# Scores of a gated recurrence in four groups of products instead of eight, norm rows as one product, and mixer work moved from GpSimd to VectorE and ScalarE

## The chip, the cores and the metric

One core of one Trainium2 chip runs the kernel. The metric is the device time of one execution in microseconds, and the median of several runs is compared.

## What is computed

One inference step of a trunk of two layers, with a width of 1024, on 512 prompt tokens and 8 sample tokens. Each layer is a feed-forward block, a mixer of three parallel branches and a second feed-forward block, each with a norm before and after it. The change touches the mixer, above all its first branch (HGRN2, 4 heads of 128x128), and the norms:

```python
def gla_chunked(q, k, v, logf, s0):      # per head: S_t = diag(f_t) S_{t-1} + k_t v_t^T ; o_t = S_t^T q_t
    rel = jnp.where(mask, b[:, :, None] - b[:, None, :], -jnp.inf)   # b: running sum of logf in a chunk
    scores = jnp.einsum('bthk,btshk,bshk->btsh', qc, jnp.exp(rel), kc)
    o_intra = jnp.einsum('btsh,bshv->bthv', scores, vc)
    S_new = jnp.exp(b_last)[..., None] * S + jnp.einsum(
        'bshk,bshv->bhkv', kc * jnp.exp(b_last[:, None] - b), vc)
o = o * lax.rsqrt(jnp.mean(o * o, axis=-1, keepdims=True) + EPS)     # then the norm's gain and silu(xg)

def decoder_layer(x, ...):
    h = rms_norm(x, norm_g[0]);  x = x + 0.5 * rms_norm(swiglu(h, ...), norm_g[1])
    h = rms_norm(x, norm_g[2]);  proj = h @ w_in
    a_out = hgrn2_mixer(...);  b_out = gmlp_mixer(...);  c_out = s5_mixer(...)
    merged = sum of sigmoid gates * (branch @ w_branch);  x = x + rms_norm(merged @ w_out, norm_g[3])
    h = rms_norm(x, norm_g[4]);  x = x + 0.5 * rms_norm(swiglu(h, ...), norm_g[5])
```

The score of tokens t and s is a sum over the 128 key channels of q_t, k_s and the product of all forget gates f between s and t.

## The kernel before

**Layout.** Channels lie on the partitions and the 520 tokens on the columns, in two halves of 256 and 264. Each large product runs as three TensorE products on a high and a low part of both operands (`mm3`, lines 117 to 120). A weight unit of 128x1024 is loaded by SyncE into `raw`, cast to `whi` by ScalarE (L98), and its rest `wlo` is formed by VectorE (L102) or, with `share=True`, by GpSimd through `ptt` (L232).

**Order.** Each engine runs its instructions in order. The long products are the main line of the program; the recurrences are generators (`side`) that are moved on one step whenever `tick(us)` has counted enough time of products (3.1 us a step for a head, 2.0 us for the S5 scan). The chains of the four heads of a layer follow one another. The framework then lays the instructions out by its own estimates, so that the order on an engine isn't quite that of the text.

**A head** (`hgrn_operands`, `hgrn_head`). The projections give f, q and g, with two VectorE operations that scale f and k (L1003, L1004), and a GpSimd product for `sg`. The chain then makes the scores A: first the diagonal (L1030, L1031), then seven levels of doubling distance. Each level has four fp32 products of 64 columns (L1088), a GpSimd product that moves k on (L232), a VectorE product that moves q on (L1091) and a masked copy of 256 columns into A (L1092). The products T of the gates come from GpSimd. Between the levels, `load` brings the sample states of two tokens, `state` updates them with three GpSimd products (`st`, `vb`), and `output` multiplies them with q (L1071). After the levels come the transposes of k (L1106), the states (L1111), the output (L1123, L1125) and the norm of o.

**Norms.** `stat` sums squares with one-column products (L256, L258), `rstd` takes nine small VectorE steps (L220 to L228), and `rows` spreads the result over 128 partitions with two or three fp32 products (L270), one for each 128 tokens. There are 12 calls for the norms after a block, 12 for those before one, and 16 for the heads.

**S5 scan and gelu.** Each of 8 scan steps splits two products of 512 columns: VectorE takes one half, GpSimd the other (L812 to L835). `gelu2` takes three VectorE operations (L244, L245, L247).

## Time and profile before

| | us |
|---|---|
| median of 3 runs | 2754.24 |
| lowest and highest | 2752.72, 2756.12 |
| profiled execution, its own time | 2757.39 |
| span of its instructions | 2755.3 |
| VectorE, ScalarE, GpSimd busy in it | 1557.5, 1014.9, 795.2 |
| first mixer's heads 0 to 3 | about 480 to 700 from the start |
| second mixer's | about 1825 to 2045 from the start |

PE is TensorE's products, PEld its weight loads, DVE VectorE, ACT ScalarE, POOL GpSimd, SPq SyncE's queue. In a row of grouped instructions stand line, engine, operation, out<-in with shapes and count, then busy us and mean ns of one, then the idle time before them and what ended it. In a row in order of time stand start, length, engine, line and tiles, and in brackets the idle time before it. An fp32 product appears as two records, and a row with x8 is eight records; records overlap, so the pace is the length less one record, divided by seven. In a row by stretches stand the length and, for PE, PEld, DVE, ACT and POOL, busy time and number of instructions, then the granted share of TensorE's clock, the DMA share and GB/s. In a row of waits stand total, number and longest.

### The profile page before, as it was taken

The page shows a single profiled execution, that of the slowest core. Times are in us where ns is not written, and L with a number is a line of the kernel's source. Part 1 is how long each engine was busy: PE and PEld are TensorE (multiplying, and loading weights), DVE is VectorE, ACT ScalarE, POOL GpSimd, SP SyncE. Part 2 cuts the span into 40 slices and gives each one's busy share as a digit, 9 for nine tenths or more (in the row PEclk, how much of TensorE's full clock was granted, in tenths as well). Part 3 has the DMA queues.
Part 4 walks back from the last instruction along what each step waited for, and adds up shares of the span by engine and source line. Part 5 has one row for each costly group of instructions (what it writes and reads, how often), then busy time and mean ns, then how long its engine had stood idle before and what let it go on. Part 6 is the DMA issues. An engine that isn't in the chain of part 4 may idle for free. (4 is left out here: it accounts for less than half of the span.)

```text
span 2755.3 us, 54254 instructions
## 1 busy us (share of the span) xinstructions
PE 2673.8 (97%) x21976; PEld 2649.0 (96%) x21976; DVE 1557.5 (57%) x3127; ACT 1014.9 (37%) x2014; POOL 795.2 (29%) x1033
## 2 busy tenths in 40 slices
PE   7999999899999999999999999998999999999998
PEld 7999999889999999999999999998999999999998
DVE  7677867865574564344473434668555654634444
ACT  4344444333243353322343323433323334433232
POOL 5478812453221112011121101145521311301010
PEclk9999999999999999999999999999999999999999
DMA  4344543542232323232322222445332223222321
GB/s 135 102 141 148 160 135 121 182 126 83 86 93 92 116 77 93 93 92 100 93 77 93 90 95 93 131 135 156 98 100 86 87 92 120 84 89 88 99 91 54
DMA packets 131706, 291.16 MB, mean 106 GB/s; under 512 B 19024, under 2 KB 59760, under 8 KB 131456
## 3 DMA queue, kind: packets, MB, share of 16 engines
q1 hardware_dynamic: 131456, 287.70, 33.1%
q8 instruction: 173, 2.83, 0.4%
q14 instruction: 77, 0.63, 0.1%
HBM read 256.97 MB, written 30.67 MB: 104 GB/s over the span
## 5 line engine op out<-in xcount | busy, mean ns | idle before, releaser
L117 PE MATMUL mm<-h,whi 128*128 128x256 f32 (+1 forms) x4224 | 1057.9, 287 | 18.2 <-ACT h L298 7.0
L118 PE MATMUL mm<-h,wlo 128*128 128x256 f32 (+1 forms) x4224 | 1047.1, 284 | 1.1 <-DVE wlo L102 1.1
L117 PEld LDWEIGHTS mm<-h,whi 128*128 128x128 f32 x4224 | 801.6, 190 | 20.2 <-ACT h L298 7.0
L118 PEld LDWEIGHTS mm<-h,wlo 128*128 128x128 f32 x4224 | 804.0, 190 | 1.7 <-DVE wlo L102 1.6
L98 ACT CAST whi<-raw 128x1024 fp32r<-128x1024 f32 (+1 forms) x424 | 437.3, 1032 | 510.9 <-PE mm L120 432.7
L102 DVE TENSOR_TENSOR wlo<-raw,whi 128x1024 fp32r<-128x1024 f32 (+1 forms) x385 | 474.0, 1231 | 233.1 <-ACT whi L98 230.3
L120 PE MATMUL mm<-h,whi 128*128 128x256 f32 (+1 forms) x4224 | 594.5, 283 | 0.0
L120 PEld LDWEIGHTS mm<-h,whi 128*128 128x128 f32 x4224 | 543.1, 189 | 0.0
L111 POOL TENSOR_TENSOR hid<-vb,hid 128x256 fp32r<-128x256 f32 (+1 forms) x132 | 132.7, 1006 | 870.0 <-ACT hid L110 857.0
L117 PE MATMUL mm<-hid,whi 128*128 128x256 f32 (+1 forms) x1408 | 349.0, 284 | 3.6 <-ACT hid L110 3.6
L118 PE MATMUL mm<-hid,wlo 128*128 128x256 f32 (+1 forms) x1408 | 347.5, 283 | 0.0
L124 DVE TENSOR_TENSOR va<-mm,r 128x256 f32<-128x256 f32 (+1 forms) x320 | 136.1, 426 | 310.3 <-PE mm L120 304.0
L117 PEld LDWEIGHTS mm<-hid,whi 128*128 128x128 f32 x1408 | 265.6, 189 | 3.8 <-ACT hid L110 3.8
L118 PEld LDWEIGHTS mm<-hid,wlo 128*128 128x128 f32 x1408 | 266.2, 189 | 0.0
L120 PE MATMUL mm<-hid,whi 128*128 128x256 f32 (+1 forms) x1408 | 201.2, 283 | 0.3 <-DVE hid L111 0.3
L124 DVE TENSOR_TENSOR vb<-mm,r 128x256 f32<-128x256 f32 (+1 forms) x176 | 74.9, 425 | 192.5 <-PE mm L120 192.5
L120 PEld LDWEIGHTS mm<-hid,whi 128*128 128x128 f32 x1408 | 182.7, 189 | 0.5 <-DVE hid L111 0.5
L110 ACT CAST hid<-vb 128x256 fp32r<-128x256 f32 (+1 forms) x176 | 72.1, 410 | 280.4 <-DVE vb L403 277.1
L232 POOL TENSOR_TENSOR wlo<-raw,whi 128x1024 fp32r<-128x1024 f32 x39 | 94.8, 2432 | 226.5 <-ACT whi L98 226.5
L401 ACT ACTIVATE sil<-va 128x256 f32<-128x256 f32 (+1 forms) x176 | 73.7, 419 | 152.8 <-DVE va L124 149.1
L434 DVE TENSOR_TENSOR y<-mm,y 128x264 f32<-128x264 f32 (+1 forms) x128 | 54.2, 425 | 117.1 <-PE mm L120 116.6
L403 DVE TENSOR_TENSOR vb<-vb,sil 128x256 f32<-128x256 f32 (+1 forms) x176 | 83.6, 475 | 17.2 <-ACT sil L401 2.5
(462 smaller groups left out, 3792.2 us busy)
## 6 DMA issues: line engine op xcount, KB each, us to landing
raw<-in_w_up SPq DMA_DIRECT2D x176, 512.0 KB, 3.7
raw<-in_w_in SPq DMA_DIRECT2D x88, 512.0 KB, 3.6
raw<-in_w_down SPq DMA_DIRECT2D x64, 448.0 KB, 3.4
raw<-in_w_down SPq DMA_DIRECT2D x32, 512.0 KB, 3.5
tab<-tb SPq DMA_DIRECT2D x48, 256.0 KB, 2.3
tab<-tab SPq DMA_DIRECT2D x48, 256.0 KB, 3.4
raw<-in_w_branch SPq DMA_DIRECT2D x24, 512.0 KB, 3.7
raw<-in_w_out SPq DMA_DIRECT2D x16, 512.0 KB, 4.6
```

The source lines that it names most:

```text
L98: nc.scalar.copy(hi[:, :n], raw[:, :n])
L102: nc.vector.tensor_tensor(lo[:, :n], raw[:, :n], hi[:, :n].bitcast(F32), ALU.subtract)
L110: nc.scalar.copy(pair[:, 0], src)
L111: (lo_eng or nc.gpsimd).tensor_tensor(pair[:, 1], src, pair[:, 0].bitcast(F32), ALU.subtract)
L117: mm(out, wh, x[:, 0], start=first and k == 0, stop=False)
L118: mm(out, wl, x[:, 0], start=False, stop=False)
L120: mm(out, wh, x[:, 1], start=False, stop=last and k == n - 1)
L124: self.nc.vector.tensor_tensor(dst, p, self.rms(half), ALU.mult)
L232: self.nc.gpsimd.tensor_tensor(out, a, b, op)
L401: nc.scalar.activation(s, a, AF.Silu)
L403: nc.vector.tensor_tensor(b, b, s, ALU.mult)
L434: nc.vector.tensor_tensor(ys, pd, ys, ALU.add)
```

## The change

Seven things change; lines that only carry a new name are left out.

1. The scores come from four groups (the diagonal with level 0, then c = 2, 8, 32) instead of eight. Each group multiplies k with a widened q of 192 columns per 128 tokens (128 tokens and six segments), four products to a group, in two PSUM tiles. Masked copies go in three pieces per tile.
2. q, k and the segments are moved on by VectorE and ScalarE (`segments`, `shift`); the products T stay on GpSimd.
3. The sample states are scaled by ScalarE and added up by VectorE, one token at a time; loads are issued two steps ahead of their use.
4. `rows` is one product of 256 or 264 columns with a matrix of ones; its operand `diag` is made by VectorE in `stat`. The heads' 1e-6 is added to the sums, not to the squares.
5. Units of the mixer, halves of the S5 products, the low parts of a, b and c, and `sg` go from GpSimd to VectorE; the scaling of f and k goes from VectorE to ScalarE.
6. `gelu2` takes two VectorE operations instead of three.
7. A head's blocks run in the order q, g, f, and f has one buffer; score buffers share the memory of the norm's sums.

```diff
     def stat(self, acc, half, mean, col=None, eps=None):
...
+        diag = self.tmph("diag", half, 1)
+        self.nc.vector.tensor_tensor(diag[:, :HT].rearrange("p (i t) -> p i t", i=2),
+                                     self.ident[:, None].to_broadcast([P, 2, P]),
+                                     col[:, :2, None].to_broadcast([P, 2, P]), ALU.mult)
+        if half:
+            self.nc.vector.tensor_scalar(diag[:, HT:], self.ident[:, :NS], col[:, 2:3], None, ALU.mult)
     def rows(self, s):
-        for i in range(2 + half):
-            n = P if i < 2 else NS
-            self.nc.tensor.matmul(r[:, 128 * i:128 * i + n], col[:, i:i + 1].to_broadcast([P, P]), self.ident[:, :n],
-                                  start=True, stop=True)
+        self.nc.tensor.matmul(r, self.ones.to_broadcast([P, P]), diag, start=True, stop=True)
     def gelu2(...):
-        nc.vector.tensor_scalar(t, t, GELU_A, 1.0, ALU.mult, ALU.add)
-        nc.vector.tensor_tensor(t, t, x, ALU.mult)
+        nc.vector.scalar_tensor_tensor(t, t, 1.0, x, ALU.add, ALU.mult)
     def s5_scan(...):            # twice in a step
-            self.ptt(tc_[:, 1], wp[:, 1], si[:, 1], ALU.mult)
-            v.tensor_tensor(tc_[:, 0], wp[:, 0], si[:, 0], ALU.mult)
+            v.tensor_tensor(tc_, wp, si, ALU.mult)
     def hgrn_operands(...):
-            v.tensor_scalar(fs, fs, lb1, lb, ALU.mult, ALU.add)
-            v.tensor_scalar(ks, ks, lb1, None, ALU.mult)
+            nc.scalar.activation(fs, fs, AF.Identity, scale=lb1, bias=lb)
+            nc.scalar.activation(ks, ks, AF.Copy, scale=lb1)
     def hgrn_head(...):
+        def scores(keys, qv):
+            w = SEGS * 32
+            for i in (0, 2):
+                pt = self.pxt()
+                for e in range(2):
+                    nc.tensor.matmul(pt[:, w * e:w * e + w], til(keys, i + e), qv[:, i + e], start=True, stop=True)
+                yield A[:, i:i + 2], pt[:, :2 * w].rearrange("p (e n) -> p e n", e=2)
+        def segments(n):
+            nc.scalar.copy(sb[:, :, 0:2], qb[:, :, 2:4])
+            nc.scalar.copy(sb[:, :, 2], qb[:, :, 1])
+            v.tensor_tensor(sb[:, :, 3::2], qb[:, :, 2:4], bc(fb[:, :, 1:3], 2), ALU.mult)
+            v.tensor_tensor(sb[:, :, 4], sb[:, :, 5], fb[:, :, 1:2].to_broadcast([P, G, c]), ALU.mult)
+        def shift(n):
+            v.tensor_tensor(qb[:, :, c:], sb[:, :, 2 * c:5 * c], fb[:, :, 0:1].to_broadcast([P, G, 3 * c]), ALU.mult)
+            v.tensor_tensor(kb[:, :, 0::2], kb[:, :, 0::2], fb[:, :, 1::2][:, :, :, None].to_broadcast([P, G, 2, c]), ALU.mult)
+            v.tensor_tensor(kh, kh, f2[:, :, 1:2].to_broadcast([P, G, 2 * c]), ALU.mult)
+        def put(n, a, pt):
+            for b, s, m in ((2, 0, 2), (1, 2, 3), (3, 5, 1)):
+                v.copy_predicated(av[:, :, :, b * c:(b + m) * c],
+                                  mv[:, None, :, s * c:(s + m) * c].to_broadcast([P, 2, 32 // c, m * c]),
+                                  pv[:, :, :, s * c:(s + m) * c])
         def state(b0):
-            self.ptt(st, st, bc(fs), ALU.mult)
-            self.ptt(vb, vb, bc(ks), ALU.mult)
-            self.ptt(st, st, vb, ALU.add)
+            for b in range(2):
+                nc.scalar.activation(st[:, b], st[:, b], AF.Copy, scale=fs[:, b0 + b:b0 + b + 1])
+                v.scalar_tensor_tensor(st[:, b], vb[:, b], ks[:, b0 + b:b0 + b + 1], st[:, b], ALU.mult, ALU.add)
-        for lev in range(7):
...
+        for n in range(-1, 3):
+            if n < 0:
+                for a, pt in scores(k, q0):
+                    v.tensor_tensor(a, pt[:, :, :P], self.ident[:, None].to_broadcast([P, 2, P]), ALU.mult)
+                    v.copy_predicated(a.rearrange("p i (b two) -> p i b two", two=2)[:, :, :, 1],
+                                      self.mask[:, None, :64].to_broadcast([P, 2, 64]), pt[:, :, P:])
+            else:
+                for a, pt in scores(k, room[n]):
+                    put(n, a, pt)
+            if n >= 0:
                 output()
             yield
+            if n < 0:
+                qp, kp, fp = pair(q), pair(k), pair(f)
+                v.tensor_tensor(qp[:, :, 1], qp[:, :, 1], fp[:, :, 0], ALU.mult)
+                v.tensor_tensor(kp[:, :, 0], kp[:, :, 0], fp[:, :, 1], ALU.mult)
+            else:
+                shift(n)
+            if n < 2:
+                segments(n + 1)
+            if n in (0, 1):
+                load(2 * n + 4)
+            state(2 * n + 2)
+            yield
```

## Rows read from the trace of the kernel before

**Rows 1.** The page's first lines: span; each engine's busy us, share and instructions.

```profile
span 2755.3 us, 54254 instructions
PE 2673.8 (97%) x21976; PEld 2649.0 (96%) x21976; DVE 1557.5 (57%) x3127; ACT 1014.9 (37%) x2014; POOL 795.2 (29%) x1033
```

**Rows 2.** Busy time by stretches: first mixer, a feed-forward stretch, second mixer.

```profile
500.00:550.00 50.00, 43.83 (x337) 42.16 (x336) 48.89 (x107) 19.00 (x44) 27.71 (x50) 0.97 0.63 196
550.00:600.00 50.00, 46.44 (x369) 44.05 (x368) 38.83 (x100) 16.50 (x46) 30.82 (x52) 0.97 0.40 118
600.00:650.00 50.00, 47.82 (x372) 46.80 (x371) 25.20 (x58) 17.60 (x36) 23.83 (x35) 0.93 0.33 95
...
1100.00:1150.00 50.00, 50.00 (x419) 50.00 (x418) 14.43 (x16) 16.56 (x29) 1.76 (x2) 1.00 0.29 99
...
1850.00:1900.00 50.00, 43.07 (x333) 41.64 (x332) 47.62 (x108) 18.87 (x45) 25.80 (x46) 0.97 0.62 194
```

**Rows 3.** What TensorE waited for, in the whole span: total us, times, longest.

```profile
PE aux L270 <- DVE rcol L228: 7.1, 6, 2.9
...
PE aux L1106 <- POOL k L232: 4.6, 6, 1.4
...
PE aux L270 <- DVE col L228: 3.7, 3, 1.8
...
PE aux L1088 <- POOL k L232: 3.6, 2, 2.0
```

**Rows 4.** TensorE in order of time: fp32 products of 160, 144 and 64 columns.

```profile
199.72 0.43 PE L682 MATMUL aux<-rc,ei 128*128 128x160 f32 x2
199.99 0.43 PE L682 MATMUL aux<-rc,er 128*128 128x160 f32 x2
...
543.61 1.14 PE L790 MATMUL aux<-y,tab 128*128 128x144 f32 x8
...
544.90 1.08 PE L1088 MATMUL aux<-q,k 128*128 128x64 f32 x8
```

**Rows 5.** All score products of the seven levels, grouped by line and form.

```profile
L1088 PE MATMUL aux<-q,k 128*128 128x64 f32 x448 | 59.1, 276 | 7.6 <-POOL k L232 3.6 <-DVE q L1091 2.2 <-DVE sil L244 1.3
```

**Rows 6.** In order of time near 600 us: two GpSimd rows, then TensorE's wait.

```profile
601.23 0.61 POOL L232 TENSOR_TENSOR st<-st,fs 128x256 f32<-128x256 f32 x1 [3.21 <-DMA st<-in_state_hgrn]
...
603.25 1.61 POOL L232 TENSOR_TENSOR k<-k,TT 128x256 f32<-128x256 f32 x1
...
604.91 1.97 PE L1088 MATMUL aux<-q,k 128*128 128x64 f32 x8 [1.60 <-POOL k L232]
```

**Rows 7.** VectorE in order of time, two back-to-back pairs: 1024 and 256 columns.

```profile
544.20 1.21 DVE L102 TENSOR_TENSOR wlo<-raw,whi 128x1024 fp32r<-128x1024 f32 x1
545.33 0.42 DVE L124 TENSOR_TENSOR va<-mm,r 128x264 f32<-128x264 f32 x1
...
549.12 0.41 DVE L1091 TENSOR_TENSOR q<-q,TT 128x256 f32<-128x256 f32 x1
549.45 0.42 DVE L1092 COPY_PREDICATED A<-mask,aux 128x256 f32<-128x256 uint8 x1
```

**Rows 8.** A norm in order of time: a GpSimd unit and a VectorE step.

```profile
461.39 2.38 POOL L232 TENSOR_TENSOR wlo<-raw,whi 128x1024 fp32r<-128x1024 f32 x1 [4.27 <-ACT whi L98]
...
462.18 1.62 DVE L221 TENSOR_SCALAR rcol<-rcol 128x3 f32<-128x3 f32 x1
...
463.83 0.16 DVE L222 TENSOR_TENSOR rs_s<-rcol 128x3 f32<-128x3 f32 x1
```

**Rows 9.** VectorE by line and form, first mixer (480 to 960 us).

```profile
L1091 DVE TENSOR_TENSOR q<-q,TT 128x256 f32<-128x256 f32 x24 | 11.7, 489 | 10.4 <-PE aux L1088 10.4
...
L812 DVE TENSOR_TENSOR ta<-w,tab 128x512 f32<-128x512 f32 x7 | 5.8, 830 | 7.9 <-ACT w L792 7.9
L244 DVE TENSOR_SCALAR sil<-sil 128x144 f32<-128x144 f32 x16 | 5.6, 347 | 0.0
```

**Rows 10.** What GpSimd waited for, the loads of the sample states and values.

```profile
POOL st L232 <- DMA st<-in_state_hgrn: 16.1, 8, 3.6
POOL vb L232 <- DMA vb<-vd: 15.6, 12, 3.1
```

More of the change, by code (lines that the diff above doesn't have):

```diff
@@ L260, in stat @@
             col = self.tmpt("col", 4, 4)[:, :n]
-        self.rstd(col, v[:, :n])
-        return v, col, half
+        m = v[:, :n]
+        if eps is not None:
+            m = self.tmpt("rs_v", 2, 4)[:, :n]
+            self.nc.vector.tensor_scalar(m, v[:, :n], eps, None, ALU.add)
+        self.rstd(col, m)
+        diag = self.tmph("diag", half, 1)
[4 more added lines that the diff above has]
+            self.nc.vector.tensor_scalar(diag[:, HT:], self.ident[:, :NS], col[:, 2:3], None, ALU.mult)
+        return v, diag, half
     def rows(self, s):
-        v, col, half = s
+        v, diag, half = s
         r = v[:, 128:128 + HW[half]]
-        for i in range(2 + half):
-            n = P if i < 2 else NS
-            self.nc.tensor.matmul(r[:, 128 * i:128 * i + n], col[:, i:i + 1].to_broadcast([P, P]), self.ident[:, :n],
-                                  start=True, stop=True)
+        self.nc.tensor.matmul(r, self.ones.to_broadcast([P, P]), diag, start=True, stop=True)
         return r
@@ L282, in norm_rows, with acc_tiles, acc_room, acc2_room @@
         self.defer(1, go)
-    def acc_tile(self):
-        return self.tmpt("acc", 3)
+    def acc_tiles(self):
+        acc = self.acc_room()
+        return [acc[:, half] for half in (0, 1)]
+    def acc_room(self):
+        return self.tmp.tile([P, 3, TW], F32, tag="acc", name="acc", bufs=1)
+    def acc2_room(self):
+        return self.tmp.tile([P, 2, TW], F32, tag="acc2", name="acc2", bufs=1)
     def new_h(self):
@@ L716, in mixer_units @@
     def mixer_units(self, l):
-        return [lambda i=i, m=m: self.unit(self.t["w_in"][l, m], 8, 128, share=i % 2 == 0) for i, m in enumerate((0, 1, 2, 3, 8))]
+        return [lambda i=i, m=m: self.unit(self.t["w_in"][l, m], 8, 128) for i, m in enumerate((0, 1, 2, 3, 8))]
     def ffn_units(self, l, f):
@@ L1138, in hgrn_head @@
         for half in (0, 1):
-            st = self.stat(sqs[half], half, self.mean_h)
+            st = self.stat(sqs[half], half, self.mean_h, eps=1e-6)
             yield
@@ L1310, in start @@
                 self.pre_lo(0, 0, half, j)
-            acc = self.sq_sum([self.x[j][:, SL[half]] for j in range(KD)])
-            self.defer(1 + half, lambda: self.norm_rows(acc, half))
+            self.sq_sum(accs[half], [self.x[j][:, SL[half]] for j in range(KD)])
+            self.defer(1 + half, lambda: self.norm_rows(accs[half], half))
         self.new_h()
+        accs = self.acc_tiles()
         up = lambda m: tuple(self.unit(t["w_up"][0, 0, m, :, k], 8, 128) for k in range(2))
@@ L1416, in lay_out @@
     s, u = np.arange(P)[:, None], np.arange(P)[None]
-    w = lambda k: u[:, u[0] >> k & 1 == 1]
-    o["level_mask"] = f(np.stack([((s ^ w(k)) >> k == 1) & (w(k) > s) for k in range(7)], 1).astype(np.float32))
+    odd = u[:, u[0] & 1 == 1]
+    masks = [odd == s + 1 - (s & 1) * 2]
+    for c in (2, 8, 32):
+        col = np.arange(SEGS * 32)
+        key = 4 * (col // (SEGS * c)) + np.array([a for _, a in PAIRS])[col // c % SEGS]
+        masks.append(s // c == key[None])
+    o["level_mask"] = f(np.concatenate(masks, 1).astype(np.float32))
     o["tri_mask"] = (u >= s).astype(np.float32)
```

118 lines of the change are left out of this document (61 added, 57 removed).

## The prediction

> **What bounds the kernel now.** I read the engines' shares first: TensorE is busy 2673.8 of 2755.3 us, no other engine over 57% [rows 1]. So time can only come from two places: TensorE's own work, and the 81.5 us in which it is idle plus whatever it loses to a lower clock. Next, the stretches of 50 us show where the losses lie. In a feed-forward stretch TensorE issues 419 products at full clock; in the heads' stretches (500 to 650, and the same in the second layer from 1850) it issues 333 to 372, is busy 43 to 48 of 50 us, and the granted clock drops to 0.93 to 0.97, that is, part of the time it runs at 1.2 instead of 2.4 GHz after gaps [rows 2]. VectorE is full there: 48.89 of 50 us from 500 to 550, 38.83 from 550 to 600; ScalarE has two thirds free [rows 2]. Third, TensorE's waits: 4.6 and 3.6 us end with a GpSimd k, 7.1 and 3.7 us with the last step of a norm on VectorE [rows 3]. Fourth, one such wait in order of time: GpSimd stands 3.21 us for a state's load, does three state products, then k takes 1.61 us, and TensorE has waited 1.60 us at 604.91 [rows 6]. The time is therefore the sum of TensorE's work outside the heads' stretches and, inside, of TensorE's work and of stalls that come from VectorE's and GpSimd's queues.
>
> **Score products.** Before, a head has 28 products of 64 columns and 4 of 128 (two records each, 64 records). The 64-column records follow at (1.08 - 0.276)/7 = 0.115 us [rows 4, 5]; I give the 128-column ones the same. That is 7.4 us a head. After, there are 16 products of 192 columns, 32 records. No such width is in the trace. A 144-column record takes (1.14 - 0.286)/7 = 0.122 us (taking 0.286 for one record) and a 160-column one 0.27/2 = 0.135 us [rows 4], both 0.847 ns a column, so my estimate for 192 is 0.163 us. Bounds: not under 0.135, the 160-column price; not over 0.163 + 0.115 = 0.28 if a weight load no longer hid behind the product before it, which the 144-column pace speaks against. I take 0.163: 5.2 us a head, 2.15 us saved, over 8 heads 17.2 us. The first head of each layer runs where VectorE is full, so I count half of it there: **-15 us** (bounds: -24 with 0.135, +12 with 0.28).
>
> **Norm rows.** 40 calls. Half 0: four records of 128 columns, 0.46 us, become two of 256, 0.43 us. Half 1: two more of 8 columns, 0.46 to 0.69 us, say 0.58, become two of 264, 0.45 us. Over 20 pairs **-3.2 us**. In front of that stands `diag`, one VectorE operation of 256 columns (0.42 us from start to end [rows 7]) and in half 1 a small one (0.16 us, the length of a small step [rows 8]): about 0.5 us on a path for which TensorE waited in 9 of the 24 calls outside the heads (6 and 3 waits [rows 3]). 9 x 0.5 = 4.5 us; the other 15 have slack, bound 24 x 0.5 = 12, below nothing if stalls on that path leave. One such stall is in rows: L221 takes 1.62 us where its neighbour takes 0.16, and it ends at 463.80, as the GpSimd unit beside it does (461.39 + 2.38) [rows 8]; the second layer repeats it. Those units now go to VectorE, where one may lie in front of the same step for 1.13 us [rows 7]. I take **+3 us**.
>
> The Trainium skill ("SBUF — State Buffer", section "Who interferes with whom") says that a VectorE operation in a two-port mode, or with two SBUF inputs, and a GpSimd operation hold a shared port pair as a lock, the later one blocked to the end. The trace agrees at 463.80. By that rule every such loss goes with GpSimd's products; what this would give is the first rival below.
>
> **VectorE's work.** Two pairs give its pace: 1.13 us for 1024 columns, 0.33 for 256 [rows 7], so about 0.06 us + 1.04 ns a column (estimate from these). Per head go: seven q products and seven masked copies (0.33 each), the 512-column diagonal (0.59), four scalings of f and k and two of the squares (at most 0.33): 7.2 us. Come: two diagonals of 256 and two odd-column copies of 128 (1.04), two pair products (0.66), 18 masked copies of 192, 128 and 64 columns (3.5), six segment products (1.56), nine shifts of 384 and 256 (3.4), eight state sums of 128 (1.5), diag, eps, two splits and two sg (2.2): 13.8 us, +6.6. The level operations measured 0.489 us beside GpSimd against 0.41 alone [rows 7, 9]; with that gone, about +5.4. A scan step pays +0.53 us for two products of 512 instead of 256 columns, and saves two L244 of 0.347 us and about 0.15 us on L812 (0.830 [rows 9] against 0.68 for 512 columns alone): -0.3, and down to -1.2 if its seven smaller operations also lose their GpSimd waits. In the full stretch of a layer (500 to 600) lie two heads, six scan steps and about two units of 1.13 us: +10.8 to 13.2, -2 to -7, +2.3, so +6 to +13.5 us against 1.1 + 11.2 = 12.3 us free [rows 2]. It just fits; I add nothing for it, and this is the sum's weakest place. Splits of b and c, the other gelu savings and later heads fall where VectorE is half idle [rows 2]: nothing, as long as that cover stays.
>
> **Stalls.** k no longer waits in GpSimd's queue: 4.6 + 3.6 = 8.2 us of waits [rows 3] can go, and the clock's loss after them, (0.03 + 0.03 + 0.07) x 50 = 6.5 us in the first layer's three stretches [rows 2], 13 with the second. In their place comes VectorE: scores wait for shift and segments (about 1.7 us by the pace above, behind the masked copies). I take a third of 21.2: **-7 us**, bounds -21 and 0.
>
> **Loads and ScalarE.** GpSimd stood 16.1 + 15.6 us for sample loads [rows 10]; these waits move to ScalarE (state) and VectorE (values), and the weight casts and evacuations queue behind them. But a load is now issued two steps ahead of its use, not one (3.1 us more of products), so I expect most of it gone. ScalarE takes some 19 more operations a head, about 5 us over a head's 45 us, beside 16.5 to 19 of 50 busy [rows 2]: hidden. Uncovered, a cast comes late and with it a unit.
>
> **Sum.** -15 - 3.2 + 3 - 7 = -22.2 us. The profiled execution took 2757.39 us (span 2755.3), 3.15 over the median of the runs shown. 2757.39 - 22.2 = 2735.2 profiled, so about **2732 us** for the median.
>
> **Rivals.** *GpSimd was the limit of the chains.* Then all 21.2 us of stalls and clock leave: -15 - 3.2 + 3 - 21 = -36, **2718 us**. For it: k ends the waits, and GpSimd is busy back to back in them [rows 3, 6]. Against: VectorE is as full [rows 2], and T stays on GpSimd.
> *The saving is hidden.* The chain's latency, not TensorE's work, sets the pace of the heads, so shorter products only lengthen gaps; only the last head of each layer, beside the gates, pays 2 x 2.15: -4.3 - 3.2 + 3 = -4.5, **2750 us**. For it: gaps in every head's stretch [rows 2]. Against: TensorE is still 88 to 96% busy there.
> *VectorE overflows* (the other sign). Place: 500 to 600 of each layer. Price: each operation waits for the one before it and takes its length, 0.09 us over the pace; 35 more operations a head make 3.1 us, so two heads add 2 x (6.6 + 3.1), the units 2.3, the scan -2: 19.7 us against 12.3 free, 7.4 us of new stalls a layer, 15 in all. Heads there save nothing: 15 - 8.6 - 3.2 + 3 = +6, **2760 us**. It decides from about 17 us added to that stretch of a layer; below that the savings elsewhere still win.
> The Trainium skill ("Perfetto Trace Analysis", section "Optimizing Scalar/DVE Operations") speaks against this change: with VectorE saturated, work may be moved off it, even to GpSimd. VectorE's 48.89 of 50 us is such a stretch; the rule's result is this third rival.
>
> **How the numbers follow.** Chances: forecast 0.52, GpSimd's limit 0.20, hidden 0.15, overflow 0.13. 0.2% (5.5 us) is about what a measurement of this kernel can tell from no change. Forecast and first rival are faster: 0.72; hidden: same, 0.15; overflow: slower, 0.13. The range runs from 2714, just under the first rival, to 2760, which takes in the hidden case and half of the overflow. The forecast's own range, by the stalls' and norms' bounds, is 2718 to 2748.
>
> **What would show it.** Right: 256 score records instead of 512 at about 0.163 us pace; no wait of TensorE on a GpSimd k; VectorE at 48 to 50 of 50 us from 500 to 550 and TensorE at over 45; L221 at 0.17 us; L270 waits some 0.5 us longer. Wrong: score records near 0.28 us; new waits of TensorE on shift, segments or masked copies of several us; VectorE or ScalarE idle for sample loads; or the clock still at 0.93 in the heads' third stretch, which would put the loss elsewhere.

## The result, and the profile after

The changed kernel takes **2704.23 us** (median of 4 runs, 2703.20 to 2705.28), the kernel before in the same session 2755.18 (2752.72 to 2757.23): ratio 0.9814, 95% interval [0.9802, 0.9826]. It gains 51 us where I forecast 22; the time lies below the range (2714 to 2760), and below the first rival too (2718).

The changed kernel's page, first lines (columns as in [rows 1]):

```profile
span 2702.8 us, 53557 instructions
PE 2640.5 (98%) x21600; PEld 2615.5 (97%) x21600; DVE 1597.4 (59%) x3421; ACT 1062.8 (39%) x2166; POOL 573.1 (21%) x772
```

Against [rows 1] VectorE has 40 us more, GpSimd 222 us less, TensorE 33 us less. Where these lie shows in the two mixers. Stretches of the kernel before, the first and the second mixer (columns as in [rows 2]):

```profile
460.99:985.90 524.91, 507.54 (x4152) 498.06 (x4151) 311.88 (x670) 183.14 (x372) 173.23 (x251) 0.99 0.37 111
1805.53:2331.01 525.48, 507.16 (x4152) 497.88 (x4151) 311.40 (x670) 183.02 (x372) 174.16 (x251) 0.99 0.36 111
```

The same two of the changed kernel:

```profile
459.75:959.32 499.57, 491.81 (x3999) 483.56 (x3999) 329.31 (x800) 206.26 (x446) 69.16 (x123) 1.00 0.37 117
1778.39:2277.63 499.24, 492.04 (x4000) 483.63 (x4000) 329.47 (x800) 206.31 (x446) 68.88 (x123) 1.00 0.37 117
```

The mixers became 25.3 and 26.2 us shorter, 51.6 together; all the rest of the program changed by less than 1 us. In the mixers TensorE's idle time fell from 35.7 to 15.0 us (1050.4 - 1014.7 and 998.8 - 983.9), so by 20.7. Its busy time fell by 30.8 us, of which the shorter score products are 17.6 (below); the other 13 are the norm rows, at most 2, and products that no longer run at the low clock: by the trace the granted clock was 0.50 in 27.3 us of the two mixers before and is so in 6.8 us now, which is a loss of 13.7 us before and of 3.4 now.

The stretches of [rows 2] in the changed kernel:

```profile
500.00:550.00 50.00, 45.25 (x349) 43.59 (x348) 47.03 (x130) 23.78 (x63) 9.21 (x20) 1.00 0.59 187
550.00:600.00 50.00, 49.98 (x398) 48.02 (x397) 46.09 (x141) 25.67 (x70) 10.94 (x26) 1.00 0.43 126
600.00:650.00 50.00, 49.66 (x402) 49.10 (x402) 37.62 (x106) 22.46 (x52) 3.37 (x7) 1.00 0.38 127
...
1850.00:1900.00 50.00, 47.86 (x372) 45.36 (x372) 45.98 (x141) 25.58 (x71) 13.15 (x28) 1.00 0.47 146
```

This is the puzzle of the case. VectorE is fuller than before in the sum of the first two (93.1 against 87.7 us), and yet TensorE stalls less and its clock stays at 1.00, that is 2.4 GHz, where it was 0.93 to 0.97.

What TensorE waited for, changed kernel, whole span (total us, times, longest):

```profile
PE aux L279 <- DVE diag L272: 6.2, 4, 2.4
...
PE aux L279 <- DVE diag L268: 3.2, 3, 1.4
...
PE aux L1073 <- DVE k L1101: 1.6, 2, 0.9
...
PE aux L858 <- issue: 1.3, 4, 0.5
```

No wait on a GpSimd k is left; the 8.2 us of [rows 3] became 1.6 on VectorE's k. A wait that I had not listed went too. The S5 scan's products waited 7.4 us for something that the profile doesn't show ("issue"), and wait 1.3 now (line 858). In the kernel before, whole span:

```profile
PE aux L847 <- issue: 7.4, 4, 2.4
```

### The profile page after: what moved, and what is told of

It reads as the page before. It is cut to its first block, busy times and chain, and to the rows that moved or that the text cites. A ratio compares the mean times of both kernels' runs of the same rounds, so it can differ in the third digit from the quotient of the medians.

```text
span 2702.8 us, 53557 instructions
## 1 busy us (share of the span) xinstructions
PE 2640.5 (98%) x21600; PEld 2615.5 (97%) x21600; DVE 1597.4 (59%) x3421; ACT 1062.8 (39%) x2166; POOL 573.1 (21%) x772
## 4 chain that ended last, share of the span: by engine, by line
PE 80%; issue 7%; DVE 6%; POOL 4%; DMA 2%; ACT 1%; SPq 0%; DVEq 0%; POOLq 0%; ACTq 0%
PE mm L122 24%; PE mm L125 24%; PE mm L123 24%; PE mm L956 1%; PE mm L958 1%; PE mm L957 1%; DMA raw<-in_w_in 1%; PE aux L1073 1%; PE aux L279 1%; PE aux L257 1%; PE aux L695 0%; DVE h L317 0%; DVE acc L218 0%; PE aux L803 0%; DMA x<-in_xT 0%
## 5 line engine op out<-in xcount | busy, mean ns | idle before, releaser
L107 DVE TENSOR_TENSOR wlo<-raw,whi 128x1024 fp32r<-128x1024 f32 (+1 forms) x399 | 486.7, 1220 | 243.8 <-ACT whi L103 240.1
L129 DVE TENSOR_TENSOR va<-mm,r 128x256 f32<-128x256 f32 (+1 forms) x320 | 136.0, 425 | 279.9 <-PE mm L125 274.9
L958 PE MATMUL mm<-whi,h 128*128 128x256 f32 (+1 forms) x320 | 90.5, 283 | 0.0
```

Source lines behind the costliest of these rows:

```text
L107: nc.vector.tensor_tensor(lo[:, :n], raw[:, :n], hi[:, :n].bitcast(F32), ALU.subtract)
L129: self.nc.vector.tensor_tensor(dst, p, self.rms(half), ALU.mult)
L958: nc.tensor.matmul(p, self.h[k][:, 1, tk], wh, start=False, stop=k == KD - 1)
```

## The experiments

Each batch was timed beside the kernel before on its own chip (2755.2 to 2757.4 us there). Two rows from different batches compare to some 5 us, and the framework lays out the first 105 us a little differently for each kernel, which by itself moves the time by up to 6 us. Line numbers are those of each kernel. The last column of the table I worked out from the traces, and call it **VectorE held up**: for each VectorE instruction that overlaps a GpSimd one, its length less the median length of the same operation and shape where it overlaps none, summed over the whole span where it is over 25% longer.

| kernel | us | ratio to before, interval | VectorE held up, us |
|---|---|---|---|
| before | 2756 | | 152.2 |
| changed kernel | 2704.2 | 0.9814 [0.9802, 0.9826] | 91.4 |
| scores only | 2736.6 | 0.9928 [0.9913, 0.9943] | 152.0 |
| moves only | 2710.8 | 0.9842 [0.9826, 0.9859] | 91.9 |
| rows as before | 2696.6 | 0.9782 [0.9768, 0.9797] | 91.0 |
| changed, idle products | 2833.6 | 1.0278 [1.0263, 1.0294] | 93.9 |
| rows as before, spare products | 2721.0 | 0.9870 [0.9854, 0.9886] | 132.6 |
| rows as before, spare copies | 2702.8 | 0.9803 [0.9789, 0.9818] | 110.6 |
| changed, k back | 2711.6 | 0.9839 [0.9818, 0.9860] | 97.2 |
| changed, S5 halves and gelu back | 2711.0 | 0.9833 [0.9817, 0.9848] | 103.6 |
| changed, states back | 2722.4 | 0.9874 [0.9857, 0.9890] | 109.5 |
| changed, units back | 2741.2 | 0.9945 [0.9929, 0.9961] | 108.3 |
| changed, units back in four pieces | 2724.8 | 0.9888 [0.9873, 0.9902] | 100.9 |
| before, k moved alone | 2743.1 | 0.9958 [0.9943, 0.9973] | 151.9 |
| before, states moved alone | 2741.4 | 0.9946 [0.9930, 0.9963] | 134.0 |
| before, units moved alone | 2763.5 | 1.0031 [1.0020, 1.0042] | 136.0 |
| before, S5 halves and gelu alone | 2758.3 | 1.0013 [1.0002, 1.0024] | 144.2 |

The two theories were: **late results** (what GpSimd owes comes late because of other work in its queue) and **held up** (VectorE can't run while a GpSimd product runs, whoever needs its result). Both can act at once.

### Scores only

The changed kernel with all its moves, its norm rows and its gelu put back, so that the four-group scores are left, with k moved on by GpSimd. The new order of a head's blocks, the earlier loads, and what VectorE and ScalarE do to q and its segments stay in it too.

```diff
-        for lev in range(7):                  # four products of 64 columns each
+        for n in range(-1, 3):                # four products of 192 columns each
...
+            g.tensor_tensor(kb[:, :, 0::2], kb[:, :, 0::2], fb[...], ALU.mult)
+            g.tensor_tensor(kh, kh, f2[...], ALU.mult)
```

> The kernel after with everything but the four-group scores put back: old norm rows, states, S5 halves, splits, sg and units on GpSimd, f and k scaled by VectorE, three-operation gelu, and k of the new scores moved by GpSimd. If the gain beyond the products (about 32 of 51 us) came from fewer rounds in the chain: 2715 to 2725 us. If it came from taking work off GpSimd, only the products' 16 us are left: 2737 to 2745 us, with TensorE's waits on a GpSimd k still there.

Measured 2736.57 us, 20 below before. About 6 us of it arise in the first 105 us, ahead of every score: the framework lays the start out another way. The score products do what I had worked out. Groups of the changed kernel by line and form, and one row of eight records:

```profile
L1073 PE MATMUL aux<-q,k 128*128 128x192 f32 x128 | 24.2, 332 | 2.1 <-DVE k L1101 1.6 <-ACT q L1053 0.3
L1073 PE MATMUL aux<-acc,k 128*128 128x192 f32 x128 | 23.8, 326 | 0.0
```

```profile
548.74 1.46 PE L1073 MATMUL aux<-acc,k 128*128 128x192 f32 x8
```

These are 256 records, at a pace of (1.46 - 0.326)/7 = 0.162 us (0.163 was my estimate): 32 of them are 5.2 us a head against 7.4, 17.6 us in eight heads. One thing that I expected didn't come: the view of this kernel's waits shows none of TensorE on a GpSimd k. The 8.2 us of [rows 3] went with the seven levels, and the kernel still takes 32 us more than the changed one, so those waits alone can't be what the moves bring.

### Moves only

The kernel before with its seven levels and its norm rows, but everything moved off GpSimd that the change moves, and its other two moves (f and k scaled by ScalarE, gelu). Core lines:

```diff
-            self.ptt(kv, kv, Tr, ALU.mult)
+            v.tensor_tensor(kv, kv, Tr, ALU.mult)
...
-            self.ptt(st, st, bc(fs), ALU.mult)
-            self.ptt(vb, vb, bc(ks), ALU.mult)
-            self.ptt(st, st, vb, ALU.add)
+            for b in range(2):
+                nc.scalar.activation(st[:, b], st[:, b], AF.Copy, scale=fs[:, b0 + b:b0 + b + 1])
+                v.scalar_tensor_tensor(st[:, b], vb[:, b], ks[:, b0 + b:b0 + b + 1], st[:, b], ALU.mult, ALU.add)
```

> The kernel before with its seven levels and its norm rows, but all two-input work of the mixers taken from GpSimd as in the change (k of each level, states, S5 halves, splits, sg, units), f and k scaled by ScalarE, two-operation gelu. If the stalls came from GpSimd's work: 2755 - 30 = about 2722 to 2728 us. If they came from the number of rounds: 2745 to 2755 us. If VectorE overflows with seven levels on it: over 2755 us.

Measured 2710.8 us, 11 below the range that I had named for GpSimd's work: the moves alone bring 45.7 of the 51 us. Its page, first lines, and its stretches from 500 on:

```profile
span 2708.4 us, 54112 instructions
PE 2656.4 (98%) x21976; PEld 2637.3 (97%) x21976; DVE 1564.9 (58%) x3217; ACT 1046.7 (39%) x2110; POOL 581.2 (21%) x779
```

```profile
500.00:550.00 50.00, 48.81 (x404) 47.90 (x404) 46.82 (x123) 23.48 (x61) 10.84 (x24) 1.00 0.64 191
550.00:600.00 50.00, 48.05 (x398) 46.01 (x397) 41.81 (x111) 23.16 (x59) 11.94 (x24) 1.00 0.41 126
```

For the same products TensorE's idle time is 52.0 us instead of 81.5, and its busy time 2656.4 instead of 2673.8 [rows 1]. VectorE has 46.82 of 50 us where it had 48.89 with less to do [rows 2]. The moves, which I had counted at 7 us (the stalls) and feared (VectorE's work), are nearly the whole gain.

### Norm rows as before

```diff
-        diag = self.tmph("diag", half, 1)
-        self.nc.vector.tensor_tensor(diag[:, :HT]..., ALU.mult)
...
-        self.nc.tensor.matmul(r, self.ones.to_broadcast([P, P]), diag, start=True, stop=True)
+        for i in range(2 + half):
+            n = P if i < 2 else NS
+            self.nc.tensor.matmul(r[:, 128 * i:128 * i + n], col[:, i:i + 1].to_broadcast([P, P]), self.ident[:, :n],
+                                  start=True, stop=True)
```

> The kernel after with the norm rows as before (two or three fp32 products, no diag, eps added to the squares). My terms were -3.2 us for the products and +3 us for diag on the path: 2701 to 2707 us either way, 2704 if both terms were right; over 2710 if the rows were a part of the unexplained gain, under 2700 if diag costs more than the products give.

Measured 2696.55 us (2695.31 to 2698.30), 7.7 below the changed kernel, and the fastest of all: **the one-product rows cost time**, and the changed kernel without them beats both kernels. Its waits for the norm's last step, whole span:

```profile
PE aux L301 <- DVE col L237: 3.7, 3, 1.8
...
PE aux L301 <- DVE rcol L237: 2.6, 4, 0.6
```

That is 6.3 us against 9.4 on `diag`; 2.5 us more lie in the first 105 us, where they may be no more than another layout. By the times at which the same products start in the two kernels, the other 4 to 5 us arise behind the heads, some 2 us in each layer; I could not place all of them. TensorE does save something on the rows themselves, but in half 1 alone (from the first record to the fourth product after it 1.13 us before, 0.90 now; in half 0 0.81 and 0.88).

### Idle products on GpSimd

The changed kernel with products of a constant tile by itself, whose values nobody needs, put into the mixers' text.

```diff
+        for _ in range(2 * n):
+            self.nc.gpsimd.tensor_tensor(self.tri, self.tri, self.tri, ALU.mult)
```

> The kernel after, plus two-input products on GpSimd on a 128x128 mask of ones and zeros (times itself, value unchanged), two for each 256-column product that the change took from it in scan, states, moves of k, splits and sg (units excepted); no other engine waits for them until the masks are used in the second branch. If GpSimd's products slowed VectorE by holding SBUF reads from it: VectorE operations in the heads at 0.5 us and more, 2715 to 2735 us. If only the results of GpSimd's queue were late: 2704 to 2708 us.

Measured 2833.59 us, 129 more than the changed kernel, but it doesn't tell the theories apart. The products waited for little, and the framework laid them out in heaps: 232 of the 496 in the first 250 us, in front of the low parts of the trunk's units, and 248 at the end of the first mixer (800 to 960). TensorE waited 27.8 us on such a GpSimd low part, and 52.8 on VectorE's `va`. By itself it shows what a queue full of ready work does. Group by line and form:

```profile
L248 POOL TENSOR_TENSOR tri<-tri 128x128 f32<-128x128 f32 x496 | 235.3, 474 | 173.9 <-DVE ws L1332 138.0
```

### Spare products, and spare copies

The kernel with the rows as before gets GpSimd products that can't run early: each reads a value that the mixer has just written (five after a sample output, two in a scan step, 192 in all), and nobody reads what it writes.

```diff
+    def spare(self, col, n):
+        for _ in range(n):
+            self.nc.gpsimd.tensor_tensor(self.scr..., col[:, :, None].to_broadcast([P, 2, P]), e, ALU.mult)
...
+            self.spare(sample_o[:, b0:b0 + 2], 5)
```

> The changed kernel with the norm rows as before (2696.6 us) plus GpSimd products of 256 columns with two SBUF inputs, 0.5 to 0.6 us each, whose result nobody reads: five after each sample output of a head and two in each step of the S5 scan, each made ready by data that has just been written, so that they can't run early. Nothing waits for GpSimd's result, so if the gain of the moves came from results that were late in GpSimd's queue, the time stays within 4 us of 2696.6. If it came from VectorE being held up while a GpSimd product runs, VectorE's products with two inputs get longer beside them (256 columns 0.42 to over 0.6 us) and the time rises by 10 us or more.

Measured 2720.96 us, **24.4 more**, with no change of any work that TensorE needs. GpSimd's other results now stand behind the spare products, but little of the price shows there: TensorE's waits that end with GpSimd rise from 0.7 to 3.2 us. Then the same with one input each:

```diff
-            self.nc.gpsimd.tensor_tensor(self.scr..., col[:, :, None].to_broadcast([P, 2, P]), e, ALU.mult)
+            self.nc.gpsimd.tensor_copy(self.scr..., col[:, :, None].to_broadcast([P, 2, P]))
```

> As the kernel with the 192 spare GpSimd products (2721.0 us against 2696.6 without them), but each spare product is a copy of one input: same places, same data waited for, same 256 columns written. In the traces so far VectorE's operations keep their length beside a GpSimd copy and get longer beside a GpSimd product of two SBUF inputs. If that is the whole price, the copies cost 0 to 5 us: 2696 to 2702. If any work in GpSimd's queue costs (results behind it that come late, order, traffic), it stays at 2715 to 2725.

Measured 2702.81 us, 6.3 more, a little over what I had allowed the held-up theory (0 to 5) and far from the 18 or more that any work in the queue should have cost. VectorE's second product of k, by line and form, in the kernel without spare work, with products and with copies:

```profile
L1145 DVE TENSOR_TENSOR k<-k,TT 128x256 f32<-128x256 f32 x24 | 10.0, 417 | 0.0
```

```profile
L1155 DVE TENSOR_TENSOR k<-k,TT 128x256 f32<-128x256 f32 x24 | 16.7, 696 | 0.0
```

```profile
L1155 DVE TENSOR_TENSOR k<-k,TT 128x256 f32<-128x256 f32 x24 | 12.1, 503 | 0.0
```

The same 24 instructions take 417, 696 and 503 ns each. VectorE instructions beside a spare one are held up by 40.5 us in the kernel with products and by 11.2 in that with copies (over the whole span the table has 41.6 and 19.6 more), and the kernels lost 24.4 and 6.3 us: some 0.6 us of time for each us that VectorE is held up with the products, 0.3 to 0.6 with the copies. Copies are not free, though I had expected it from the short ones (4 to 32 columns) of the earlier traces. The second layer's stretch, without spare work, with products, with copies:

```profile
1850.00:1900.00 50.00, 48.44 (x382) 46.21 (x381) 45.20 (x139) 26.24 (x71) 10.61 (x24) 1.00 0.46 146
```

```profile
1850.00:1900.00 50.00, 40.22 (x304) 36.99 (x305) 47.52 (x112) 22.79 (x63) 31.48 (x47) 1.00 0.50 150
```

```profile
1850.00:1900.00 50.00, 46.61 (x368) 44.26 (x367) 46.59 (x132) 24.57 (x66) 21.32 (x46) 1.00 0.49 148
```

With the products VectorE finishes 112 instructions instead of 139 in the same stretch while its busy time goes up by 2.3 us, and TensorE drops by 8.2 us: this is what [rows 2] showed at 1850, without my seeing it (47.62 us busy with 108 instructions). A VectorE that looks full can be one that stands beside GpSimd.

### Single parts given back

From the changed kernel, one part at a time went back to GpSimd. First k, then the S5 halves with the three-operation gelu:

```diff
-            v.tensor_tensor(kb[:, :, 0::2], ...)
-            v.tensor_tensor(kh, kh, ...)
+            g.tensor_tensor(kb[:, :, 0::2], ...)
+            g.tensor_tensor(kh, kh, ...)
```

> The changed kernel (2704.2 us) with only the moves of k in the four-group scores, two products per group, back on GpSimd. Late results: waits of TensorE on a GpSimd k return (4 to 8 us of them in all) and with the clock after them the time rises by 8 to 20 us. Holding up: GpSimd has some 50 products more, 25 to 40 us of work, about a sixth of what was taken from it, so the time rises by a sixth of 45 us, about 7 us, and VectorE's operations beside them are longer.

```diff
-            v.tensor_tensor(tc_, wp, si, ALU.mult)
+            self.ptt(tc_[:, 1], wp[:, 1], si[:, 1], ALU.mult)
+            v.tensor_tensor(tc_[:, 0], wp[:, 0], si[:, 0], ALU.mult)
...
```

> The changed kernel (2704.2 us) with the halves of the S5 products back on GpSimd and the gelu in three VectorE operations. My prediction counted this part at nothing. If most of what I missed in the stalls was the scan (TensorE's wait for the scan's first product was 7.4 us before and is 1.3 us after), the time rises by 8 us or more and that wait returns; if it was only the heads' k, it rises by at most 3 us.

Measured +7.4 and +6.8 us; the intervals overlap that of the changed kernel, so either is known to some 6 us. With k back TensorE waits only 0.5 us on a GpSimd k, not the 4 to 8 us of late results, so the +7.4 fits the held-up theory's number (7); for the scan the answer lies between the two that I had named (8 or more, 3 at most), and the scan's wait, 1.3 us in the changed kernel, is 3.6. Then the states:

```diff
-            for b in range(2):
-                nc.scalar.activation(st[:, b], st[:, b], AF.Copy, scale=...)
-                v.scalar_tensor_tensor(st[:, b], vb[:, b], ks..., st[:, b], ALU.mult, ALU.add)
+            self.ptt(st, st, bc(fs), ALU.mult)
+            self.ptt(vb, vb, bc(ks), ALU.mult)
+            self.ptt(st, st, vb, ALU.add)
```

> The changed kernel (2704.2 us) with the three state products of each pair of tokens back on GpSimd, 0.6 us and 256 columns each, behind their loads. My prediction named GpSimd's waits for these loads (31.7 us before) as what stood in front of k. Without k in that queue, late states delay only the sample outputs: 2704 to 2707. If the products' holding up of VectorE is what counts, 96 products more cost about 96/190 of what the 190 spare products cost (24 us), some 12 us: 2712 to 2720.

Measured +18.1 us. No k stands behind them any more, so my prediction's mechanism (k late behind a state's load) would give 0 to 3; it is as much as the held-up time grows (18.1), and above what I had named for it (8 to 16). And the low parts of the mixers' units, seven in a layer:

```diff
-        self.tok_proj("w_i", l, hh, evac)
+        self.tok_proj("w_i", l, hh, evac, hh == 0)
...
```

> The changed kernel (2704.2 us) with the low parts of the mixers' shared weight units back on GpSimd, 2.4 us each there against 1.2 us on VectorE. By my prediction VectorE is full in the first heads and these units cost it time, so giving them back should help or do nothing (2698 to 2706). If GpSimd's work holds VectorE up, or the low part comes late in GpSimd's queue, the time rises by 5 us or more; TensorE's waits on a low part then tell the second from the first.

Measured **+37.0 us**, the largest of all, from 14 instructions of 2.4 us. The view of TensorE's waits shows none on a GpSimd low part, and that was to tell late low parts from holds. What one does is seen at the first norm of a layer. GpSimd, VectorE and TensorE of this kernel, each in order of time:

```profile
463.38 2.39 POOL L241 TENSOR_TENSOR wlo<-raw,whi 128x1024 fp32r<-128x1024 f32 x1 [4.19 <-ACT whi L107]
467.36 2.46 POOL L241 TENSOR_TENSOR wlo<-raw,whi 128x1024 fp32r<-128x1024 f32 x1 [1.59 <-ACT whi L107]
```

```profile
463.80 2.00 DVE L230 TENSOR_SCALAR rcol<-rcol 128x3 f32<-128x3 f32 x1
...
467.54 2.30 DVE L291 TENSOR_SCALAR diag<-ident,rcol 128x8 f32<-128x8 f32 x1
```

```profile
469.90 1.25 PE L304 MATMUL aux<-diag,ones 128*128 128x264 f32 x2 [3.70 <-DVE diag L291]
...
471.17 0.42 PE L127 MATMUL mm<-h,wlo 128*128 128x264 f32 x1
471.39 0.42 PE L126 MATMUL mm<-h,whi 128*128 128x264 f32 x1
```

Two steps of 3 and 8 columns take 2.00 and 2.30 us, and end when the GpSimd units end (465.77, 469.82). TensorE waits 3.70 us, and after that its records of 264 columns follow at 0.22 us (471.17 to 471.39) instead of 0.12 until 474.5; the granted clock is 0.50 there, that is 1.2 GHz. In the changed kernel the same step takes 0.17 us (VectorE in order of time):

```profile
460.94 0.17 DVE L226 TENSOR_SCALAR rcol<-rcol 128x3 f32<-128x3 f32 x1
```

By the times at which the same products start in the two kernels, this norm step costs 6.2 us in the first layer and 5.3 in the second; most of the rest arises from there to the end of the heads. One loss there is no hold-up: near 599 ScalarE stood 5.4 us for a weight unit's load that came behind stores of S5 states in SyncE's queue, its cast stood in front of a score copy on ScalarE, and TensorE waited 3.2 us. To tell a long hold from a late result, the same units in four products each:

```diff
-            self.ptt(lo[:, :n], raw[:, :n], hi[:, :n].bitcast(F32), ALU.subtract)
+            for j in range(0, n, n // 4):
+                e = j + n // 4
+                self.ptt(lo[:, j:e], raw[:, j:e], hi[:, j:e].bitcast(F32), ALU.subtract)
```

> As the kernel with the mixers' seven shared units a layer back on GpSimd (2741.2 us), but each low part in four products of 256 columns instead of one of 1024. GpSimd has the same work and its result is ready no earlier. If the price of 37 us is mainly that one product of 2.4 us holds up a VectorE step of a norm or a chain for all of its length, holds are now at most some 0.6 us and the time falls to 2710 to 2725. If it is that low parts come late, or that units stand longer in their buffers so that the next load is late, it stays at 2736 or above.

Measured 2724.8 us: GpSimd has slightly more work, each low part is ready no earlier, and 16.4 of the 37 us are gone. VectorE and TensorE in order of time, the two norm steps and the product behind them:

```profile
460.07 0.36 DVE L232 TENSOR_SCALAR rcol<-rcol 128x3 f32<-128x3 f32 x1
...
463.47 0.23 DVE L293 TENSOR_SCALAR diag<-ident,rcol 128x8 f32<-128x8 f32 x1
```

```profile
463.75 0.71 PE L306 MATMUL aux<-diag,ones 128*128 128x264 f32 x2 [1.26 <-DVE diag L293]
```

TensorE waits 1.26 us there instead of 3.70, and the norm step costs 1.5 and 1.4 us in the two layers instead of 6.2 and 5.3. The other 20.6 us stay; this run doesn't say of what kind they are.

For k, the scan, the states and the units the time rises by 1.3, 0.6, 1.0 and 2.2 us for each us that the held-up time rises. So that sum shows where a cost may lie; it isn't a price.

### Single parts moved alone

The other way round, from the kernel before, one part at a time.

```diff
-            self.ptt(kv, kv, Tr, ALU.mult)
+            v.tensor_tensor(kv, kv, Tr, ALU.mult)
```

> The kernel before (2756.5 us) with one change alone: k of the seven levels moved on by VectorE. My prediction put the stalls down to k's place in GpSimd's queue: 8.2 us of waits and up to 13 us of clock, so -8 to -21 us by that reading, and a rise if VectorE overflows. If k was only where a delay of all GpSimd's work came out, the waits change their name and the time falls by less than 8 us.

Measured -13.3 us: within what my prediction gave for k's place in GpSimd's queue (-8 to -21), and the held-up time hardly moves (151.9). So late results are real for k with seven levels.

```diff
-            self.ptt(st, st, bc(fs), ALU.mult)
...
+                nc.scalar.activation(st[:, b], st[:, b], AF.Copy, scale=fs[:, b0 + b:b0 + b + 1])
+                v.scalar_tensor_tensor(st[:, b], vb[:, b], ks[:, b0 + b:b0 + b + 1], st[:, b], ALU.mult, ALU.add)
```

> The kernel before (2756.4 us) with one change alone: the sample states scaled by ScalarE and added up by VectorE, in place of three GpSimd products a pair of tokens. Taking these products away again from the changed kernel's side cost 18 us. If the moves add up, it gives about -18 us; if VectorE has room for work only once the other GpSimd products are gone too, as for the units alone (+7 us), it gives between -8 and +8 us.

Measured -16.1 us against its own batch. This one can't tell the theories apart, since in the kernel before k stands behind the states.

```diff
-        self.tok_proj("w_i", l, hh, evac, hh == 0)
+        self.tok_proj("w_i", l, hh, evac)
...
```

> The kernel before (2756.5 us) with one change alone: the low parts of the mixers' seven shared units a layer on VectorE. By my prediction this costs VectorE 2.3 us in a full stretch and saves the held-up norm step, so it should give -4 to +4 us. If the norm steps, the clock after them and the chains behind are what the units on GpSimd cost, it gives -15 to -37 us.

Measured **+7.1 us**: the same edit that is worth 37 us as the last step makes the kernel slower as the first. I had allowed +4 at most. Its waits, whole span:

```profile
PE aux L1110 <- POOL k L1112: 8.6, 5, 3.8
```

The waits of the scores on a GpSimd k rise from 3.6 [rows 3] to 8.6 us, and the clock is 0.93 in all three stretches from 500 to 650. By the times at which the same products start, this kernel is 6.4 us ahead of the kernel before when the first layer's heads begin (494 us) and 2.5 us behind when they end: it gains up to the heads and loses in them, though the held-up time of the whole span is 16 us less. My reading, which no run shows by itself, is that VectorE, held up beside GpSimd's k and states as before, now has the units as well.

```diff
-            self.ptt(tc_[:, 1], wp[:, 1], si[:, 1], ALU.mult)
-            v.tensor_tensor(tc_[:, 0], wp[:, 0], si[:, 0], ALU.mult)
+            v.tensor_tensor(tc_, wp, si, ALU.mult)
...
```

> The kernel before (2757 us) with one change alone: the halves of the S5 products on VectorE and the gelu in two VectorE operations. My prediction counted this at nothing, with -2 to -7 us of VectorE time in the full stretch. The single moves so far gave -13 (k), -15 (states) and +7 us (units) of the -46 of all moves. If single moves add up, this one and the low parts of a, b and c hold the missing -24: then -10 to -24. If the rest is the units' place, which only pays once the other products are gone (+7 alone, 37 when undone last), it gives -8 to 0.

Measured +1.7 us, interval +0.5 to +6.6 by the ratio: no gain. The four parts alone sum to -13.3 - 16.1 + 7.1 + 1.7 = -20.6 us, all moves together give -45.7, and taken back one by one they cost 7.4 + 18.1 + 37.0 + 6.8 = 69.3. The units show that a part's worth depends on what else has left GpSimd. How much of the missing 25 us comes from that is not shown: all moves together also hold the low parts of a, b and c, `sg` and the scaling of f and k by ScalarE, which no run moved alone.

## Why the prediction was wrong

**What bounds the kernel** stands: TensorE's work and its stalls in the heads' stretches; the whole gain lies in the mixers. Most of the signs that I had named for "right" came true, too: 256 score records at 0.162 us, no wait on a GpSimd k, TensorE at 45.25 of 50 us from 500 on (VectorE at 47.03, a little under its sign of 48), the norm step at 0.17 us, and waits for the rows that are 0.44 us longer each than with the old rows (9.4 against 6.3 us, 7 waits). They show that the mechanism acts, not how much it is worth. One sign of "wrong" came as well: ScalarE stands idle for sample loads.

**Score products** were right: 0.162 us a record against 0.163 estimated, 256 records, and from the moves alone to the changed kernel with its old rows 2710.8 - 2696.6 = 14.2 us against 15 forecast (the new block order and the earlier loads lie in that step too, and no run took them apart). The hidden-saving rival falls.

**Norm rows** were put at nothing and cost time. I summed -3.2 for TensorE and +3 for `diag`; together they cost 7.7 us, or 5.2 without the first 105 us. The step that failed is "9 x 0.5 = 4.5 us; the other 15 have slack", with the +3 that I took from it. With TensorE's saving as forecast, `diag` and what follows it cost 8.4 to 10.9 us, nearer the bound of 12 that I had named than the 3 that I took; 3.1 us of it show as longer waits. The stall at L221 that I blamed on GpSimd's unit [rows 8] was rightly blamed: it is gone (0.17 us), and came back with the units.

**VectorE's work** was counted fairly and judged badly. In the first mixer its busy time rose by 17.4 us, and by some 40 without the hold-ups (30.0 us of them before, 7.8 now); my 6.6 us a head and 1.13 a unit make 34.3 for four heads and seven units. It didn't overflow, but the cover that I named for it (12.3 us free from 500 to 600) was half of what carried it: in that stretch 14.2 us of VectorE's busy time had been hold-ups, and 0.7 are left. The overflow rival may be a real mechanism: the units moved alone fit it (+7.1). But that was with GpSimd's other products still running, and here they went at once.

**Stalls** are the step that failed and made the miss: "I take a third of 21.2: -7 us, bounds -21 and 0". The moves brought 45.7 us, more than twice the bound. The bound was made of two waits that end with a GpSimd k and of the clock in three stretches, so it could only hold what is late on GpSimd. That part alone was fairly sized: k by itself gave -13.3. Left out were the waits that end with VectorE, or with no releaser at all: 7.4 us at the scan's products became 1.3. The moves alone took 29.5 us off TensorE's idle time, where I had named 8.2. That these waits were long because VectorE was held up is what the spare products make likely (24.4 us for work that nobody needs); no run shows it wait by wait. The clock's share I had sized well: I named 13 us for the two mixers, and the changed kernel loses 10.3 us less to it there.

Even the row that I took for a queue [rows 6] is in part a hold, from the other side. VectorE in order of time, the kernel before:

```profile
602.95 1.42 DVE L102 TENSOR_TENSOR wlo<-raw,whi 128x1024 fp32r<-128x1024 f32 x1
```

GpSimd's k began 0.30 us behind this product and ended 0.49 us after it, which makes its 1.61 us; the two k products of that trace that ran with VectorE idle took 0.64 and 0.63.

**The rule that I cited and underpriced.** I had a row of it (L221, 1.62 us beside a GpSimd unit [rows 8]), the Trainium skill's rule on the shared port pair ("SBUF — State Buffer", section "Who interferes with whom"), and even a row for its size, the level products at 0.489 us instead of 0.41 [rows 9]; I used that as 0.08 us for each operation of the heads, and gave the rule's rival the bound of the named waits. The runs bear the rule out in kind. Over the 17 traces I counted VectorE instructions that began while a GpSimd product (TENSOR_TENSOR) was running, and compared each with the median of its own line and shape with GpSimd idle (those with no such median are left out):

```
VectorE instruction                     number   over 25% longer than alone
TENSOR_TENSOR, an operand in PSUM         3547    0%
SCALAR_TENSOR_TENSOR, operand in PSUM      471    0%
TENSOR_SCALAR, operand in PSUM              52    0%
COPY_PREDICATED, PSUM data, SBUF mask      468   14%
TENSOR_TENSOR, all in SBUF                4384   51%
SCALAR_TENSOR_TENSOR, all in SBUF          855   48%
TENSOR_SCALAR, all in SBUF                 517   79%
```

Of the 3068 lengthened ones in the last three rows, all but 12 ended after the GpSimd product did. Why the others kept their length, the counts don't say.

The other rule that I cited (the Trainium skill, "Perfetto Trace Analysis", section "Optimizing Scalar/DVE Operations") I cited by half: the same passage adds that work moved between VectorE and GpSimd might not help, because they share a port. The runs agree with the second half: parts given back to GpSimd cost 6.8 to 37.0 us.

**Loads and ScalarE.** I expected most of the waits for sample loads to go. They did not. The changed kernel's ScalarE, whole span:

```profile
ACT st L1127 <- DMA st<-in_state_hgrn: 28.0, 17, 3.1
```

That is about what GpSimd's 16.1 + 15.6 were [rows 10]. VectorE has no wait for a value's load. I saw no cost of it, since ScalarE is busy half of the time at most; it was not tried by itself.

What stays open: how the 37 us of the units divide between holds, late loads and order beyond the 16.4 that the four pieces took away, where some 2 us of the norm rows' price lie, and how the 45.7 us of the moves divide between late results and hold-ups: no run took the hold-ups away and left GpSimd's results late.

## What to carry to other kernels

An engine's busy time is not its work: where VectorE looks full, compare the length of one instruction beside GpSimd with that of the same one alone, sum the difference, and weigh that sum, beside the waits that carry GpSimd's name, when you price GpSimd's work. A move off GpSimd may lose as the first step and win as the last, so judge such moves as a set, and never by one at a time. For an operation that is added in front of a product for which TensorE already waits in some of its calls, plan with the upper bound: here the price came to 8 to 11 us of a bound of 12.

## What the runs showed of the hardware

- A GpSimd product of two SBUF inputs costs VectorE time even if nobody needs it: 192 of 256 columns (0.73 us each on the average for most) held VectorE up by 40.5 us and made the kernel 24.4 us slower; copies of one input in their place (0.51 us) 11.2 and 6.3 us.
- The hold runs to the end of the GpSimd instruction: steps of 3 and 8 columns took 2.00 and 2.30 us beside products of 2.39 and 2.46, and 0.36 and 0.23 us where each of these was cut into four. It acts the other way too: a GpSimd product of 0.63 us took 1.61 behind a VectorE product of 1024 columns.
- VectorE's products and scalings with an operand in PSUM were never lengthened by over 25% (0 of 4070), so that work can stay beside GpSimd. Masked copies out of PSUM, whose mask lies in SBUF, were in 14% of 468 cases.
- After a stall of TensorE of 3.70 us its products ran at a granted clock of 0.50 and half their pace for 4.6 us (469.9 to 474.5), some 2.3 us more on top of the wait.
